# First conditioning on TensorE from eight 1 MB loads, and GpSimd without splits and tables, in a decoder block on one core

## The chip, the cores and the metric

The kernel runs on one core of a Trainium2 chip. The metric is the device time of one execution in microseconds. A core has five engines that run side by side and wait for one another by semaphores: TensorE (PE in the profile, its weight loads PEld), VectorE (DVE), ScalarE (ACT), GpSimd (POOL) and SyncE (SP, which here only issues loads and stores). Each engine works through its own instructions in order. DMAs are issued from the queues of SP, ACT and POOL and are carried out by 16 shared DMA engines.

## The reference, cut to what matters

One decoder layer for 256 tokens of width 1024, everything in float32:

```
mod = silu(c) @ ada_w + ada_b                 # c: 1 row of 1024; ada_w: 1024 x 6144
shift1, scale1, gate1, shift2, scale2, gate2 = split(mod, 6)
h = rms_norm(x, norm1_g) * (1 + scale1) + shift1
proj = h @ w_in + b_in                        # w_in: 1024 x 4384
# q, kv, gates, x_m, o_pre, i/f, merge gates = split(proj)
# three attention branches over compressed, selected and window keys:
#   s = q k * 0.125 - slope * dist, slope = 2**-(head+1); softmax; gated sum
# a chunked mLSTM with causal convolution
mixed = (g_a * (o_nsa @ proj_a) + g_b * (y_ml @ proj_b)) @ w_out
x = x + gate1 * mixed
h2 = rms_norm(x, norm2_g) * (1 + scale2) + shift2
x = x + gate2 * experts(h2)                   # top 4 of 32, clamped SwiGLU, 12 MB of weights each
out = rms_norm(x, final_g)
```

The compressed branch adds a position table `cmp_pe` to blocks of 32 keys and feeds them through `w1`, gelu and `w2`.

## The kernel before, in words

The program has two stages. The **block stage** computes everything up to the routing, the **expert stage** streams the weights of all 32 experts (each in 8 tiles of 128 x 2048 for the up projection and 4 for the down projection, 1 MB each, `fetch`) through 14 buffers and multiplies them with up to 64 gathered tokens an expert. A run-time branch for experts with more tokens stands behind it and is not taken here. Some 11 expert tiles are fetched already while the block stage ends (the list `FETCH`, by round).

**Conditioning (lines 149 to 238, 986 to 1013).** The first third of `mod` (shift1 and scale1, 2048 columns) is needed before the first product. It is computed in four quarters of 256 columns each of shift and scale (`ada_quarter(b)`): eight DMAs of 256 KB a quarter bring `ada_w`, DVE accumulates weight rows times `sc = silu(c)` over eight instructions (lines 209 and 211) into `aacc`, and eight matmuls with a 128 x 128 tile of ones as the weights sum over the partitions into columns (`ada_columns`). DVE then makes `mod` and `ab` (lines 222, 224), ACT makes two of the eight blocks of `h` transposed (`rows_T`, lines 232, 233; the normalized x lies transposed in PSUM), and DVE their low parts (line 237). Quarter b thus releases product b of the first pass.

**Products by parts.** A float32 product is made of three products in the faster fp32r form: a weight tile `w` is split into `r` (rounded, ACT, line 297 or 306) and the rest `l` (line 298 or 307, on DVE, or on POOL for the steps in `POOL_SPLIT`), activations into `hh` and `hl`; `mm3` (line 49) issues r x hh, l x hh, r x hl. A *step* is one 512 KB weight tile: a load (`s_load`, 5 buffers `w`), a split (`s_split`, one step ahead), 24 matmuls of 256 columns (`s_prod`). There are 35 steps of `w_in` in nine passes (`x`, `tok`, `q`, `k`, `o`, four of merge gates), 8 of the merge (`proj_a`, `proj_b`), 8 of `w_out`.

**Beside the steps** run generators, each advanced by a piece per step: `th_mlstm`, `th_cmp` (compressed keys), eight `th_att` (POOL first multiplies the tables `neg0` and `neg1` by the slope of each head, lines 898 and 899; DVE adds them to the scores and takes the row maximum, line 913), and `th_ada` (lines 538 to 587), which computes the other four sixths of `mod` (gate1, shift2, scale2, gate2: `q4` 0 to 3): 8 tiles `wada` of 512 KB each, two buffers, one `scalar_tensor_tensor` on DVE a tile (line 570), a tile fetched when the buffer two before is free; then two matmuls with ones sum over the partitions.

**What sets the order.** In the conditioning, ACT, DVE, SP and PE follow the written order (`manual_schedule`); POOL and everything behind it are ordered by a scheduler before the run. The small rows (`row_loads`: biases, norms, convolution weights, `cmp_pe`) are issued on ACT's queue in three portions.

Of the kernel before, what the change touches and what calls it, by code (L numbers as in the profile page):

```python
# [29 lines left out]
DIRECT = 0  # L30
ADA_POOL = ()
POOL_SPLIT = {0, 1, 2, *range(5, 60, 6)}
# [3 lines left out]
def block_kernel(ctx, tc, x, c, ada_w, ada_b, norm1_g, w_in, b_in, cmp_pe_k, cmp_w1_k, cmp_w2_k,  # L36
# [32 lines left out]
    mid2 = mixed.enter_context(tc.tile_pool(name="mid2", bufs=1))  # L69
# [38 lines left out]
    for h in range(2):  # L108
        SP.dma_start(xn[:, h, :], x[0, h * 128:(h + 1) * 128, :])
# [25 lines left out]
    def load_rows(n):  # L135
        for dst, src in row_loads[:n]:
            ACT.dma_start(dst, src)
        del row_loads[:n]
# [18 lines left out]
    def conditioning():  # L157
        tp = bank_m()
        PE.transpose(tp[:, 0:8], c8, ident[:8, :8])
        ACT.activation(sg8, tp[:, 0:8], AF.Sigmoid)  # L160
        DVE.tensor_tensor(sc, sg8, tp[:, 0:8], op=OP.mult)

# [18 lines left out]

    def columns(src, r0, r1, c0):
# [5 lines left out]
    accs, last_w = {}, {}  # L188
    spare = mid2.tile([128, 4, 1024], F32, name="spare", tag="gm")

    def ada_quarter(b):
        acc = accs[b] = mid.tile([128, 2, 256], F32, name="aacc", tag=("gate1", "shift2")[b % 2])
        for j in range(4):
            if j < 2:
                w = wtile()
            elif b in (1, 2):
                w = spare[:, (b - 1) * 2 + j - 2]
            else:
                w = mid.tile([128, 1024], F32, name="wada", tag="wada", bufs=2)
            w = w.rearrange("p (f a n) -> p f a n", f=2, a=2)  # L200
            for hf in range(2):
                c0 = hf * 1024 + b * 256
                SP.dma_start(w[:, hf], ada_w[0, j * 256:(j + 1) * 256, c0:c0 + 256].rearrange("(a p) n -> p a n", p=128))
            for a in range(2):
                kt = j * 2 + a
                if kt >= KT - DIRECT:
                    last_w[b, kt] = w[:, :, a]
                elif kt == 0:
                    DVE.tensor_scalar(acc, w[:, :, a], sc[:, 0:1], None, op0=OP.mult)
                else:  # L210
                    DVE.scalar_tensor_tensor(acc, w[:, :, a], sc[:, kt:kt + 1], acc, op0=OP.mult, op1=OP.add)
            yield

    def ada_columns(b):
        p = bank_o() if b % 2 else bank_m()
        parts = [(last_w[b, kt], sc[:, kt:kt + 1]) for kt in range(KT - DIRECT, KT)] + [(accs[b], ones[:, 0:1])]
        for i, (src, v) in enumerate(parts):
            for f in range(2):
                for k in range(2):
                    mm(p[:, f * 2 + k:f * 2 + k + 1], src[:, f, k * 128:(k + 1) * 128], v, i + f + k == 0, i == DIRECT)  # L220
        ks = slice(b * 2, b * 2 + 2)
        DVE.tensor_tensor(mod[:, b], p[:, 0:4].rearrange("p (f k) -> p f k", f=2),
                          col[:, R_ADA:R_ADA + 16].rearrange("p (f k) -> p f k", f=2)[:, :, ks], op=OP.add)
        DVE.scalar_tensor_tensor(ab[:, ks], mod[:, b, 1], 1.0, col[:, R_N1 + b * 2:R_N1 + b * 2 + 2],
                                 op0=OP.add, op1=OP.mult)

    def rows_T(b):
        hTs = []
        for kt in (b * 2, b * 2 + 1):
            src = xps[kt // 2][:, (kt % 2) * 256:(kt % 2) * 256 + 256]  # L230
            hT = mid.tile([128, S], F32, name="hT", tag="hT", bufs=3)
            ACT.activation(hT, src, AF.Identity, bias=mod[:, b, 0, kt % 2:kt % 2 + 1], scale=ab[:, kt:kt + 1])
            ACT.activation(hh[:, kt, :], hT, AF.Copy)
            hTs.append(hT)
        yield
        for kt in (b * 2, b * 2 + 1):
            DVE.tensor_tensor(hl[:, kt, :], hTs[kt % 2], f32(hh[:, kt, :]), op=OP.subtract)
        yield
# [28 lines left out]
    cbias = prol.tile([128, 2, 8, 15], F32, name="cbias")  # L267
    for h in range(8):
        cs = prol.tile([128, 2, 15], F32, name="cs", tag="cs", bufs=2)
        POOL.tensor_scalar(cs, cv, 2.0 ** -(h + 1), None, op0=OP.mult)  # L270
        POOL.tensor_tensor(cbias[:, :, h, :], cs, cneg, op=OP.add)
# [497 lines left out]
    def th_cmp():  # L769
# [10 lines left out]
        for i in range(2):  # L780
# [3 lines left out]
            POOL.memset(blk[:, :, 30:32], 0.0)  # L784
            kT = kvT[:, i, :]
            for g in range(2):
# [895 lines left out]
```

## Time and profile before

| | us |
|---|---|
| median of 3 runs | 1264.95 |
| lowest and highest | 1259.71, 1265.89 |
| the profiled execution, as timed | 1260.78 |
| its span, first to last instruction | 1259.0 |
| mean granted TensorE clock | 0.979 |
| bytes read from HBM | 462.09 MB, 369 GB/s over the span |

The span lies 1.8 us under its execution's own time. A busy PE in the profile is not a PE at its peak, since matmuls are pipelined and their ends are modelled; so the rate of the DMA engines, and what an engine waited for, say more than the busy shares. Idle time of an engine that nobody waits for costs nothing.

### The profile page before, as it was taken

Reading aid. Unit: us, or ns where it says so; the run is one execution under the profiler, and the core shown is the slowest. Engines: PE = TensorE matmul, PEld = TensorE weight load, DVE = VectorE, ACT = ScalarE, POOL = GpSimd, SP = SyncE. Lnnn points to the kernel's source line nnn. Section 1 sums busy time; section 2 is a strip of 40 time slices with the busy share of each in tenths; the row PEclk is TensorE's granted clock in tenths of the full one; section 3 lists DMA queues with packets and bytes.
Section 4 is the critical chain, followed back from the end, with each engine's and each line's share of the span. In section 5 each row is a group of like instructions: output and inputs, shape, how many; then the busy total and the mean of one; then the engine's idle time right before and its main releaser. Section 6 shows DMA issues by size and latency. Waiting matters only on the chain. (4 is left out here: it accounts for less than half of the span.)

```text
span 1259.0 us, 13889 instructions
## 1 busy us (share of the span) xinstructions
PE 1139.9 (91%) x5520; PEld 537.6 (43%) x5520; DVE 391.2 (31%) x775; ACT 251.7 (20%) x477; POOL 96.9 (8%) x112
## 2 busy tenths in 40 slices
PE   3788998988999999989998999999899989998976
PEld 2787887875333334323432333333234323432222
DVE  6787795853211131112111111211121212111112
ACT  3354556431201111000100110101001100101001
POOL 6501441100000000000000000000000000000020
PEclk9898998998999999999999999999999999999999
DMA  9697737886999999999999999999999999999994
GB/s 321 171 300 237 218 104 226 301 341 252 403 419 417 418 419 418 420 421 420 419 417 419 417 419 421 420 419 419 419 420 420 420 419 418 419 419 420 423 414 177
DMA packets 116590, 465.17 MB, mean 369 GB/s; under 512 B 11442, under 2 KB 37672, under 8 KB 83624
## 3 DMA queue, kind: packets, MB, share of 16 engines
q1 hardware_dynamic: 113600, 462.20, 92.7%
q10 hardware_dynamic: 2488, 1.45, 0.4%
q0 software_dynamic: 432, 0.58, 0.3%
q8 instruction: 45, 0.74, 0.2%
q14 instruction: 25, 0.20, 0.0%
HBM read 462.09 MB, written 2.10 MB: 369 GB/s over the span
## 5 line engine op out<-in xcount | busy, mean ns | idle before, releaser
L47 PE MATMUL psup<-ww,xg 128*64 128x512 f32 x2048 | 486.4, 602 | 25.3 <-DMA ww<-in_exp_w_up 24.9
L47 PE MATMUL psdn<-ww,a 128*64 128x512 f32 x1024 | 263.5, 605 | 27.3 <-DMA ww<-in_exp_w_down 27.2
L47 PEld LDWEIGHTS psup<-ww,xg 128*64 128x64 f32 x2048 | 142.4, 136 | 322.4 <-issue 226.6
L1407 DVE TENSOR_TENSOR g<-psgt,bup 128x512 f32<-128x512 f32 x32 | 22.1, 691 | 578.3 <-PE psgt L1390 562.8
L47 PEld LDWEIGHTS psdn<-ww,a 128*64 128x64 f32 x1024 | 81.8, 138 | 182.7 <-issue 117.6
L1383 ACT ACTIVATE gu<-psup 128x512 f32<-128x512 f32 x64 | 38.3, 598 | 347.0 <-PE psup L47 347.0
L1450 DVE TENSOR_TENSOR acc<-acc,psms 128x512 f32<-128x512 f32 x56 | 38.5, 688 | 162.6 <-PE psms L47 162.6
L47 PE MATMUL psf<-hh,r 128*128 128x256 f32 x256 | 81.6, 321 | 7.1 <-ACT gm L367 5.8
L47 PE MATMUL psf<-hh,l 128*128 128x256 f32 x256 | 76.8, 301 | 0.6 <-POOL l L298 0.6
L47 PE MATMUL psf<-hl,r 128*128 128x256 f32 x256 | 76.3, 299 | 0.0
L1475 POOL TENSOR_TENSOR acc<-acc,gate 128x512 f32<-128x512 f32 x4 | 5.0, 1262 | 869.1 <-DVE acc L1450 869.1
L47 PE MATMUL psms<-G,h 128*128 128x256 f32 x256 | 66.5, 405 | 0.2 <-DVE G L1275 0.2
L47 PE MATMUL psms<-y,sc 128*128 128x512 f32 x112 | 63.0, 645 | 0.0
L47 PEld LDWEIGHTS psms<-G,h 128*128 128x128 f32 x256 | 48.2, 198 | 30.5 <-issue 24.3
L47 PEld LDWEIGHTS psf<-hh,r 128*128 128x128 f32 x256 | 52.9, 207 | 12.6 <-ACT gm L367 6.1
L1409 ACT ACTIVATE s<-g 128x512 f32<-128x512 f32 x32 | 20.2, 632 | 187.7 <-DVE g L1408 187.7
L297 ACT ACTIVATE r<-w 128x1024 fp32r<-128x1024 f32 (+2 forms) x47 | 49.2, 1046 | 42.0 <-PE psf L47 24.4
L47 PEld LDWEIGHTS psf<-hh,l 128*128 128x128 f32 x256 | 53.1, 207 | 2.7 <-issue 1.4
L47 PEld LDWEIGHTS psf<-hl,r 128*128 128x128 f32 x256 | 52.8, 206 | 0.0
L298 DVE TENSOR_TENSOR l<-w,r 128x1024 fp32r<-128x1024 f32 (+2 forms) x36 | 44.8, 1245 | 13.6 <-ACT r L297 13.2
L570 DVE SCALAR_TENSOR_TENSOR ada<-wada,sc,ada 128x1024 f32<-128x1024 f32 x32 | 41.2, 1288 | 7.7 <-DMA wada<-in_ada_w 6.6
L1313 ACT ACTIVATE xg<-psms 128x512 f32<-128x512 f32 x32 | 19.1, 598 | 111.3 <-PE psms L47 111.3
(355 smaller groups left out, 972.4 us busy)
## 6 DMA issues: line engine op xcount, KB each, us to landing
ww<-in_exp_w_up SPq DMA_DIRECT2D x256, 1024.0 KB, 19.7
ww<-in_exp_w_down SPq DMA_DIRECT2D x126, 1024.0 KB, 19.9
wada<-in_ada_w SPq DMA_DIRECT2D x32, 512.0 KB, 4.8
w<-in_w_in SPq DMA_DIRECT2D x28, 512.0 KB, 4.5
w<-in_ada_w SPq DMA_DIRECT2D x16, 256.0 KB, 4.9
w<-in_w_out SPq DMA_DIRECT2D x8, 512.0 KB, 9.3
wada<-in_ada_w SPq DMA_DIRECT2D x8, 256.0 KB, 4.7
spare<-in_ada_w SPq DMA_DIRECT2D x8, 256.0 KB, 4.2
```

The costliest lines, as they stand in the source:

```text
L47: PE.matmul(o, a, b, start=start, stop=stop, skip_group_check=True)
L297: ACT.activation(r, w, AF.Copy)
L298: (POOL if at["split"] in POOL_SPLIT else DVE).tensor_tensor(l, w, f32(r), op=OP.subtract)
L570: DVE.scalar_tensor_tensor(a, w, sc[:, kt:kt + 1], a, op0=OP.mult, op1=OP.add)
L1313: ACT.activation(XG[g][:, q * 2:q * 2 + 2].rearrange("p k e s -> p (k e s)"), p, AF.Copy)
L1383: ACT.activation(GU[e][:, b], UP[e][b], AF.Copy)
L1407: DVE.tensor_tensor(by_f(g), by_f(GT[e][0]), bias(0), op=OP.add)
L1409: ACT.activation(s, g, AF.Sigmoid, scale=1.702)
L1450: DVE.tensor_tensor(acc[:, h, ns], acc[:, h, ns], p, op=OP.add)
L1475: POOL.tensor_tensor(acc[:, h, ns], acc[:, h, ns], gate2[:, ns], op=OP.mult)
```

## The change

Nine edits:

1. The first third of the conditioning moves from DVE to PE. Eight loads of 1 MB, each 128 rows of `ada_w` x 2048 columns (8 KB in a row), go to four buffers of a pool of their own, `st`, which is closed before the pool `mid2` is opened in its place (so `gm`, `xm` and `sgo` are made later, behind the conditioning). For each, four matmuls with `sc32` (one column of `sc` repeated 32 times, 128 x 32 weights) and 512 columns of the tile go into the four 32-row parts of one PSUM bank (`ada_rows`); after eight loads, ACT and DVE copy the bank out, four PE transposes turn it, and two DVE instructions give all of `mod` and `ab` at once (`ada_columns`). All of it then stands ahead of the first product.
2. The normalized x is copied from PSUM into SBUF (`xT`), and `row_T` makes `hh` on ACT and `hT` and `hl` on DVE.
3. x is loaded by one DMA in place of two.
4. Of the small rows, two stay on ACT's queue; nine go to POOL's queue.
5. The weights `wqk` and `w2t` are issued by SP in place of ACT.
6. `POOL_SPLIT` is empty: all splits run on DVE.
7. `ADA_POOL = (3,)`: for gate2's eight tiles, ACT scales the tile in place and POOL adds it to the sum, in place of one DVE instruction.
8. The slopes leave the tables: q is scaled by 0.125 / slope as it leaves PSUM (`qsc`), the tables are added unscaled, and the slope is a constant of the DVE instruction that adds; POOL's 32 multiplications of `neg0` and `neg1` go, as do its 16 small ones for `cbias` (in their place 16 tiny memsets; two small DVE multiplications in `th_cmp`).
9. In `th_cmp`, the blocks of keys are copied by ACT (eight copies), the position table becomes a 31st column of the same matmuls, and DVE adds its result afterwards.

```diff
-DIRECT = 0
-ADA_POOL = ()
-POOL_SPLIT = {0, 1, 2, *range(5, 60, 6)}
+ADA_POOL = (3,)
+POOL_SPLIT = ()
...
-    for h in range(2):
-        SP.dma_start(xn[:, h, :], x[0, h * 128:(h + 1) * 128, :])
+    SP.dma_start(xn, x[0].rearrange("(h p) d -> p h d", p=128))
...
+    def ada_load(kt):
+        w = st.tile([128, 2, 1024], F32, name="w1", tag="w1", bufs=4)
+        SP.dma_start(w.rearrange("p f n -> p (f n)"), ada_w[0, kt * 128:(kt + 1) * 128, 0:2048])
+        ada_w1.append(w)
+
+    def ada_rows(p, kt):
+        for f in range(2):
+            for n in range(2):
+                r0 = (f * 2 + n) * 32
+                mm(p[r0:r0 + 32, :], sc32[:, kt], ada_w1[kt][:, f, n * 512:(n + 1) * 512], kt == 0, kt == 7)
+
+    def ada_columns(p):
+        rw1 = mid.tile([128, 512], F32, name="rw1", tag="gain2")
+        ACT.activation(rw1[:, 0:256], p[:, 0:256], AF.Copy)
+        DVE.tensor_copy(rw1[:, 256:512], p[:, 256:512])
+        tp = bank_m()
         for j in range(4):
...
+            PE.transpose(tp[:, j * 128:(j + 1) * 128], rw1[:, j * 128:(j + 1) * 128], ident)
...
+    def row_T(kt):
+        src = xT[0][:, kt, :]
+        hT = mid.tile([128, S], F32, name="hT", tag="hT", bufs=3)
+        ACT.activation(hh[:, kt, :], src, AF.Identity, bias=mod[:, 0, kt:kt + 1], scale=ab[:, kt:kt + 1])
+        DVE.tensor_scalar(hT, src, ab[:, kt:kt + 1], mod[:, 0, kt:kt + 1], op0=OP.mult, op1=OP.add)
+        DVE.tensor_tensor(hl[:, kt, :], hT, f32(hh[:, kt, :]), op=OP.subtract)
...
-                    DVE.tensor_tensor(blkv[lp * 64:(lp + 1) * 64, :, g, :], src, pe_, op=OP.add)
+                    ACT.activation(blkv[ls, :, g, :], src, AF.Copy)
+                pe_ = col[ls, 128 + i * 32:160 + i * 32].rearrange("p (l r) -> p l r", r=2)[:, :, lp]
+                DVE.tensor_copy(blk[ls, :, 30], pe_)
...
-        for g in range(2):
-            sl = 2.0 ** -(g * 4 + cc + 1)
-            POOL.tensor_scalar(p0[:, g], neg0, sl, None, op0=OP.mult)
-            POOL.tensor_scalar(p1[:, g], neg1, sl, None, op0=OP.mult)
...
-                DVE.tensor_tensor_reduce(out=pp[:, g], in0=psg[g][:, (0, 128)[h]:(128, 384)[h]], in1=pp[:, g],
-                                         scale=1.0, scalar=FMIN, op0=OP.add, op1=OP.max,
+                DVE.tensor_tensor_reduce(out=pp[:, g], in0=psg[g][:, (0, 128)[h]:(128, 384)[h]], in1=(neg0, neg1)[h],
+                                         scale=2.0 ** -(g * 4 + cc + 1), scalar=FMIN, op0=OP.add, op1=OP.max,
                                          accum_out=m4[:, h, g:g + 1])
...
+        load_rows(2, ACT)
+        for kt in range(4):
+            ada_load(kt)
         conditioning()
         norm_sums()
...
+        ada_kt(0)
+        ada_kt(1)
         norm_rows()
...
+        load_rows(len(row_loads), POOL)
+        for kt in range(2, KT):
+            ada_kt(kt)
         columns(rows, 0, R_X, 0)
+        for _ in range(PW):
+            s_load()
+        ada_columns(p1)
```

(`ada_kt(kt)` is `ada_rows(p1, kt)` and, for kt under 4, the load kt + 4 behind it; `sc32` is made by one DVE copy; the branch for `q4 in ADA_POOL` stood in `th_ada` before.)

PE at the start of the program, before. `psm<-ones,aacc` are the sums over partitions of a quarter, `psf<-hh,r` begins the product that the quarter releases, `psa<-ident,xn` are the transposes of x:

```order
L159 MATMUL psm<-ident,raw 128x8
L178 MATMUL psa<-ident,xn 128x128 x16
L184 MATMUL pso<-ident,raw 128x24
L47 MATMUL psm<-ones,aacc 128x1 x4
L47 MATMUL pso<-ones,aacc 128x1 x4
L47 MATMUL psf<-hh,r 128x256
L47 MATMUL psf<-hh,l 128x256
```

PE at the same place now (`w_162` to `w_253` are the eight tiles `w1`, `sc_86` is `sc32`, `rw_286` the bank that is turned):

```order
L159 MATMUL psm<-ident,raw 128x8
L46 MATMUL psf<-w_162,sc_86 32x512 x4
L46 MATMUL psf<-w_164,sc_86 32x512 x4
L179 MATMUL psa<-ident,xn 128x128 x16
L46 MATMUL psf<-w_166,sc_86 32x512 x4
...
L46 MATMUL psf<-w_253,sc_86 32x512 x4
L195 MATMUL pso<-ident,raw 128x24
L218 MATMUL psm<-ident,rw_286 128x128 x4
L46 MATMUL psf<-hh,r 128x256
L46 MATMUL psf<-hh,l 128x256
```

Two of the eight groups stand ahead of the transposes of x and six behind them, and no product stands between two quarters any more: the first waits for all eight loads.

SP's queue at the start, before:

```order
L109 DMA xn<-in_x 128x1024 x2
L203 DMA w<-in_ada_w 128x2x256 x4
L203 DMA wada<-in_ada_w 128x2x256 x4
L286 DMA w<-in_w_in 128x2x512
L203 DMA w<-in_ada_w 128x2x256 x4
L203 DMA spare<-in_ada_w 128x2x256 x4
L286 DMA w<-in_w_in 128x2x512
```

and now:

```order
L108 DMA xn<-in_x 128x2x1024
L203 DMA w_162<-in_ada_w 128x2048
L203 DMA w_164<-in_ada_w 128x2048
...
L203 DMA w_253<-in_ada_w 128x2048
L279 DMA w<-in_w_in 128x2x512 x4
L368 DMA w<-in_w_in 128x3x128
```

The first weight tiles of `w_in` moved behind all of the conditioning's loads; the last four of those wait for a free buffer at the head of the queue.

ACT in the merge, before (`sT` turns shift2, `mh` are high parts of the merged rows):

```order
L297 ACTIVATE r<-w 128x1024 x2
L1189 ACTIVATE sT<-psa 128x512
L61 ACTIVATE mh<-mt_2477 128x256
L1189 ACTIVATE sT<-psa 128x512
L61 ACTIVATE mh<-mt_2483 128x256
L297 ACTIVATE r<-w 128x1024 x2
```

and now:

```order
L290 ACTIVATE r<-w 128x1024 x2
L1190 ACTIVATE sT<-psa 128x512
L60 ACTIVATE mh<-mt_2411 128x256
L1190 ACTIVATE sT<-psa 128x512
L557 ACTIVATE wada<-wada,sc 128x1024
L60 ACTIVATE mh<-mt_2417 128x256
L290 ACTIVATE r<-w 128x1024
L557 ACTIVATE wada<-wada,sc 128x1024
```

The scaling of gate2's tiles now stands between the splits of ACT, each behind the landing of its tile; the eight additions stand together on POOL.

## Rows read from the trace of the kernel before

**Rows 1.** The page's part 2: 40 slices of the span, GB/s.
```profile
GB/s 321 171 300 237 218 104 226 301 341 252 403 419 417 418 419 418 420 421 420 419 417 419 417 419 421 420 419 419 419 420 420 420 419 418 419 419 420 423 414 177
```

**Rows 2.** Busy time by stage: stretch, us, engines with instructions, granted clock, DMA share, GB/s.
```profile
0.00:55.60 55.60, 29.12 (x148) 27.27 (x148) 38.84 (x67) 18.55 (x33) 35.47 (x63) 0.91 0.78 245
...
120.00:217.00 97.00, 89.20 (x718) 78.48 (x719) 75.28 (x237) 56.59 (x135) 29.68 (x26) 0.95 0.61 185
217.00:285.30 68.30, 60.70 (x471) 55.84 (x470) 44.36 (x57) 29.18 (x49) 7.29 (x4) 1.00 0.85 309
...
300.00:1259.00 959.00, 895.85 (x3747) 318.51 (x3745) 171.12 (x291) 111.37 (x195) 12.50 (x10) 0.99 0.99 408
```

**Rows 3.** PE in order of time, first matmuls on expert weights (start us, us).
```profile
301.17 3.65 PE L47 MATMUL psup<-ww,xg 128*64 128x512 f32 x16
```

**Rows 4.** Who waited for whom, 0 to 55.6 us: total, times, longest.
```profile
ACT hT L232 <- DVE ab L224: 17.4, 4, 6.9
```

**Rows 5.** Stretches of 10 us in the conditioning, columns as in rows 2.
```profile
20.00:30.00 10.00, 2.41 (x11) 2.44 (x12) 8.76 (x14) 2.95 (x6) 2.34 (x1) 1.00 1.08 355
...
40.00:50.00 10.00, 7.31 (x39) 7.05 (x39) 7.27 (x10) 3.73 (x8) 7.49 (x11) 0.67 0.17 44
```

**Rows 6.** In order of time: x's second half squared, x transposed, a 32-column form.
```profile
6.29 1.06 ACT L167 ACTIVATE sq<-xn 128x1024 f32<-128x1024 f32 x1 [0.21 <-DMA xn<-in_x]
...
12.82 3.46 PE L178 MATMUL psa<-ident,xn 128*128 128x128 f32 x15 [0.57 <-ACT xn L172]
...
114.25 1.08 PE L47 MATMUL psa<-cw,blk 128*32 128x128 f32 x16
```

**Rows 7.** In order of time, the first pass: product 0 begins, product 3 ends.
```profile
29.28 0.56 PE L47 MATMUL psf<-hh,r 128*128 128x256 f32 x1
...
34.33 0.28 PE L47 MATMUL psf<-hl,r 128*128 128x256 f32 x1
...
50.34 0.42 DVE L237 TENSOR_TENSOR hl<-hT,hh 128x256 fp32r<-128x256 f32 x1 [0.43 <-ACT hh L233]
51.29 1.23 DVE L298 TENSOR_TENSOR l<-w,r 128x1024 fp32r<-128x1024 f32 x1 [0.52 <-ACT r L297]
...
52.25 0.28 PE L47 MATMUL psf<-hh,r 128*128 128x256 f32 x1
...
55.28 0.28 PE L47 MATMUL psf<-hl,r 128*128 128x256 f32 x1
```

**Rows 8.** DVE and POOL in order of time; the first row has no POOL beside it.
```profile
27.87 0.75 DVE L211 SCALAR_TENSOR_TENSOR aacc<-w,sc,aacc 128x512 f32<-128x512 f32 x1
...
41.64 5.14 DVE L211 SCALAR_TENSOR_TENSOR aacc<-wada,sc,aacc 128x512 f32<-128x512 f32 x4
42.29 2.37 POOL L298 TENSOR_TENSOR l<-w,r 128x1024 fp32r<-128x1024 f32 x1 [7.12 <-ACT r L297]
...
110.21 2.83 DVE L703 TENSOR_TENSOR k<-k,wcol 128x512 f32<-128x512 f32 x1
...
266.63 1.17 DVE L1135 TENSOR_TENSOR xt<-xt,xt 128x512 f32<-128x512 f32 x1
```

**Rows 9.** What PE waited for, 55 to 300 us: total, times, longest.
```profile
PE psf L47 <- POOL l L298: 3.4, 4, 1.3
...
PE psm L47 <- DVE k L703: 2.5, 1, 2.5
```

**Rows 10.** Groups by line, 55 to 290 us: busy us, mean ns, idle before.
```profile
L298 DVE TENSOR_TENSOR l<-w,r 128x1024 fp32r<-128x1024 f32 (+2 forms) x35 | 43.6, 1245 | 13.1 <-ACT r L297 12.7 <-DMA w<-in_proj_a 0.3
...
L298 POOL TENSOR_TENSOR l<-w,r 128x1024 fp32r<-128x1024 f32 (+1 forms) x8 | 21.2, 2656 | 100.0 <-ACT r L297 72.3 <-DVE ml L62 19.8 <-DVE wcol L702 7.9
```

**Rows 11.** gate2's first and last tile on DVE, in order of time (eight in all).
```profile
223.19 1.28 DVE L570 SCALAR_TENSOR_TENSOR ada<-wada,sc,ada 128x1024 f32<-128x1024 f32 x1 [1.09 <-DMA ada<-in_ada_b]
...
259.37 1.28 DVE L570 SCALAR_TENSOR_TENSOR ada<-wada,sc,ada 128x1024 f32<-128x1024 f32 x1
```

**Rows 12.** Tile wada, 186 to 262 us: its loads' time from issue to landing.
```profile
DMA to landing us min/median/max: 3.6/6.3/8.3
```

More of the change, by code (lines that the diff above doesn't have):

```diff
@@ L180, in norm_rows @@
             xps.append(p)
+        xT.append(keep.tile([128, KT, S], F32, name="xT", tag="x8"))
+        for k2 in range(4):
+            dst = xT[0][:, k2 * 2:k2 * 2 + 2].rearrange("p k s -> p (k s)")
+            if k2 % 2:
+                DVE.tensor_copy(dst, xps[k2])
+            else:
+                ACT.activation(dst, xps[k2], AF.Copy)
+    xT = []
     def columns(src, r0, r1, c0):
@@ L185, in columns @@
         ACT.activation(col[:, c0 + r0:c0 + r1], tp[:, r0:r1], AF.Copy)
[L188 to L192, printed above, removed]
-        for j in range(4):
[L194 to L238, printed above, removed]
+    ada_w1 = []
@@ L986, in block_kernel, with ada_kt @@
     with tc.manual_schedule(engines=START):
[L987 removed]
+        load_rows(2, ACT)
+        for kt in range(4):
+            ada_load(kt)
         conditioning()
         norm_sums()
[L990 removed]
+        p1 = bank_f()
+        def ada_kt(kt):
+            ada_rows(p1, kt)
+            if kt < 4:
+                ada_load(kt + 4)
+        ada_kt(0)
+        ada_kt(1)
         norm_rows()
[L992 to L994 removed]
+        load_rows(len(row_loads), POOL)
+        for kt in range(2, KT):
+            ada_kt(kt)
         columns(rows, 0, R_X, 0)
+        for _ in range(PW):
+            s_load()
+        ada_columns(p1)
         for b in range(4):
[L997 to L1013 removed]
+            if b == 0:
+                s_split()
+            for kt in (b * 2, b * 2 + 1):
+                row_T(kt)
+            if b:
+                s_split()
+                s_prod()
+        columns(rows, R_X, NR, 0)
+        columns(rows2, 0, 64, 128)
+        DVE.tensor_tensor(bq, col[:, R_Q:R_Q + 4], qsc, op=OP.mult)
     tc.no_sync_barrier()
+    first.close()
+    mid2 = mixed.enter_context(tc.tile_pool(name="mid2", bufs=1, reuse_waits="tile"))
     gm = mid2.tile([128, 16, S], F32, name="gm", tag="gm")
+    xm = mid2.tile([128, 4, 3 + S], F32, name="xm", tag="xm")
+    DVE.memset(xm[:, :, 0:3], 0.0)
+    sgo = mid2.tile([128, 4, S], F32, name="sgo")
     for i, wm in enumerate((ml_wq, ml_wk, ml_wv)):
[L1017 removed]
+        SP.dma_start(wqk[:, i], wm[0].rearrange("h d e -> d h e"))
     for i, w2 in enumerate((cmp_w2_k, cmp_w2_v)):
[L1019 removed]
+        SP.dma_start(w2t[:, i], w2[0])
     def ml_step(k):
```

73 lines of the change are left out of this document (29 added, 44 removed).

## The prediction

> **What bounds the kernel now.** I read the page's slices first. From the eleventh slice to the last but one the DMA engines bring 403 to 423 GB/s, and before that between 104 and 341 [rows 1]. The table by stage says the same in busy shares: from 300 to 1259 us the DMA share is 0.99 at 408 GB/s, and no engine but PE is busy for more than a fifth of it [rows 2]. So the expert stage runs at the speed of its loads, and nothing in this change touches its bytes. It begins when the routing is done: the first matmul on expert weights starts at 301.17 us [rows 3]. Its fetches are held by 14 buffers, so what the block stage saves or loses ahead of that moment goes into the end of the span one to one; 0 is my term for the expert stage itself. The forecast is therefore a forecast of the start at 301.17. What lies outside the span is 1260.78 - 1259.0 = 1.8 us, and stays.
>
> In the block stage I then looked for the wait that ends last. Up to 55.6 us DVE is busy for 38.84 us, and ACT waits 17.4 us in four waits for DVE's `ab` [rows 2, 4]: the first pass is paced by DVE's weighted sums, not by loads, for in the stretch from 40 to 50 us the DMA engines bring only 44 GB/s while DVE, PE and POOL each work about 7.3 us [rows 5]. From 120 to 217 us DVE is the busiest engine besides PE (75.28 of 97 us), and from 217 to 285.3 us it has 44.36 of 68.3 us [rows 2]. PE waits for little: 3.4 us for POOL's splits and 2.5 us for the `k` of DVE are the largest waits that have to do with POOL [rows 9].
>
> **A, the conditioning and the first pass.** Removed are DVE's 32 instructions of 128 x 512, 0.75 us each where POOL is quiet; four of them beside POOL's 2.37 us split took 5.14 us instead of 3.0 [rows 8]. So one POOL instruction there cost DVE 2.14 us. Added are loads and PE work, and I follow them in order of time. x was in SBUF by 6.3 us (the second square starts there, released by the load) [rows 6]. Behind it come 8 x 1.049 = 8.39 MB; at the expert stage's 408 GB/s [rows 2] that is 20.6 us, so 26.9. The last four loads wait at the head of SP's queue for a buffer that PE must have read; two of the eight groups stand ahead of x's transposes (3.46 us and more, from 12.82) and the rest behind [rows 6], which I put at 1 us of gap: 27.9. The last group is four matmuls of 32 x 512 side by side. The nearest row is 16 matmuls of 128 columns into 32-row parts in 1.08 us [rows 6], which is the same number of columns; the first product shows PE at the slower of its two levels after idle time (0.56 us a matmul at its start, 0.28 at its end) [rows 7], so I take 2.0: 29.9. Bank copies, four transposes and two small DVE instructions are six links; `hl` and its wait for ACT, 0.42 + 0.43, stand for two of them [rows 7], so 2.6: 32.5. The split's low part, 1.23, and the first `hT` and `hl` at about 0.42 each [rows 7] make 34.6. Then four products with no quarter between them: product 0 took 34.33 + 0.28 - 29.28 = 5.3 us and product 3 took 55.28 + 0.28 - 52.25 = 3.3 [rows 7], so 5.3 + 3 x 3.3 + 0.9 for the turning of `rows` between products 2 and 3 = 16.1. The pass ends at 50.7, against 55.56 before: **-4.8**.
>
> The bounds: at the 355 GB/s of the stretch from 20 to 30 us [rows 5], which is the best that the smaller loads reached, the bytes cost 3.0 more; and all four products at the slow level cost 3 x 2.0 = 6 more. In the stretch from 40 to 50 us, where products were cut off from each other by waits, the granted clock was 0.67, between the levels of 1.2 and 2.4 GHz [rows 5]; now they follow one another, so I don't take this, and leave +4 as the upper end. If the gap is nothing, the group costs 1.08 and every product 3.3, the end is 4 us earlier: -9. The range of A is -9 to +4.
>
> Moved at no cost, with their covers: nine small rows go to POOL's queue at about 15 us and are needed when `rows` is turned near 41 us, so 20 us and more cover them; `wqk` and `w2t` go behind the weight tiles on SP, where they are first used after the first pass; `gm`, `xm` and `sgo` now lie where the tiles `w1` lay, which are free some 20 us earlier; copying PSUM to `xT` lies under the loads. If a cover were gone, each is one load's time, 3.6 to 8.3 us for a 512 KB load [rows 12].
>
> **B, splits and tables leave POOL (55.6 to 285 us).** What PE waited for because of POOL is 3.4 us for `l` and 2.5 us for `k` [rows 9]. `k` took 2.83 us beside a split on POOL, where an instruction of the same size took 0.75 alone [rows 8], so 2.1 of the 2.5 is POOL's. That is 5.5 us. In return DVE takes eight splits of 1.245 us, 10.0 us, in place of POOL's 2.656 each [rows 10]. DVE is 78% busy from 120 to 217 [rows 2], so not all of this fits in gaps; but the products now get `l` 1.4 us sooner, and the eight copies of key blocks go to ACT, which has 40 us to spare there. I put back 1.5 of the 10: **-4**. The ends: nothing comes back, -6; six tenths of the 10 lie on the path while only the waits for `l` go, +3.
>
> **C, gate2 on ACT and POOL (217 to 285 us).** DVE loses eight instructions of 1.28 us, 10.2 us [rows 11]. POOL gains eight additions of the size of a split (2.37), with two inputs from SBUF. Each may hold DVE by 2.14 us, as the four sums show, or by as little as 1.17 - 0.75 = 0.42, as `xt` shows beside a split [rows 8]: 17.1 or 3.4 us, so DVE's sum changes by +6.9 or -6.8. ACT gains eight scalings of a 128 x 1024 tile, 1.06 each by x's square [rows 6], 8.5 us on an engine with 29.18 of 68.3 us busy [rows 2]. The two ends are equally far from zero and the rows equally near: **0**, with -6 to +7.
>
> The Trainium skill, page "SBUF — State Buffer", section "Who interferes with whom", says that a DVE instruction with two SBUF inputs contends with a GpSimd instruction that reads SBUF, and that the loser is blocked for the whole of the other's instruction. The four sums, 5.14 us for 3.0, agree with it; `xt` shows less than a whole one. By that rule C would stand at its upper end wherever DVE has such an instruction to run, and the whole sum at -2.
>
> **The sum.** -4.8 - 4 + 0 = -8.8 on the profiled execution's 1260.78: 1252.0. That execution lies 0.33% under the median of the three runs, so I say **1253**.
>
> **The rivals.** (a) Every relief passes whole: A -8, B -6, C -4, so 1243. For it: the rows of the first pass show DVE as the only thing waited for. Against: PE is busy for nine tenths of the stretch from 120 us [rows 2], and takes little of what is freed. (b) POOL's additions block DVE as the four sums were blocked, C is +6.9, and the start is as forecast: 1259, which is no change. For it: DVE has 44 us to run in that stretch and the additions 8 x 2.37 = 19 us. Against: only 65% of the stretch has a DVE instruction at all. The skill's page is this rival's rule.
>
> (c) Slower: gate2's tiles pace the block stage. A tile's buffer is now held from its load through ACT's scaling and POOL's addition, and there are two. The load takes 6.3 us in the middle and 8.3 at most [rows 12], the scaling 1.06 and the addition 2.37 with DVE's hold of 2.14 before it: 11.9 to 13.9 us, so 5.9 to 6.9 a tile. Before, eight tiles stood (259.37 - 223.19) / 7 = 5.2 us apart [rows 11]. The next load waits for its buffer at the head of SP's queue, with the `w` tiles of the steps behind it, and the scaling stands in ACT's queue ahead of the splits. At 6.9 that is 7 x 1.7 = 12 us, with rival b's 6.9 on top C is +19: 1271. It makes the kernel slower than the bound below when C passes 8.8 + 6.3 = 15, or at about 6.4 us a tile with the lock whole. Against: tiles are fetched ahead of the steps, and gate2 itself is needed only at the end. (d) The change doesn't do what it says: the four matmuls of a group run one behind another. Four times 1.08 to 2.0 us (by A) is 4.3 to 8.0 us a group against 2.6 us a load; at 6.2, eight groups from 9 us on end at 58 in place of 29.9: about 1280. Against it: 16 such matmuls of 128 columns took 1.08 us, where 15 transposes of 128 columns took 3.46 one behind another [rows 6].
>
> **How the numbers follow.** Forecast 0.48 (of it 0.38 faster by over 0.5%, 0.10 within), rival a 0.18 (faster), rival b 0.18 (within), rival c 0.10 and rival d 0.03 (slower), and 0.03 within for what I haven't named. 0.5% is 6.3 us, about what a measurement of this kernel can tell from no change. Faster 0.56, same 0.31, slower 0.13. The lower ends sum to -9 - 6 - 6 = -21, 1240; the upper to +14, 1275. Leaving out rival d and most of c above, and the last of a below, 1241 to 1265 holds 8 in 10.
>
> **What would show it.** A: DMA at 400 GB/s or more up to about 27 us, the first product near 35, the last of the four near 51; wrong, if the groups of four take over 3 us or PE keeps the slow level through the pass. B: no wait of PE for POOL, `k` at 0.75, and no new wait for DVE's `l` of more than 2 us. C: DVE's instructions beside POOL's additions tell rival b by their length; waits of ACT for `wada`, or of `w` loads behind it, tell rival c. The whole: the first expert matmul near 292 instead of 301.17, and everything behind it as long as before. The prediction is wrong altogether if the expert stage's own length changes.

## The result, and the profile after

The changed kernel takes 1249.95 us in the median of four runs (1248.24 to 1251.08), the kernel before 1264.62 in the same comparison: a ratio of 0.989, with a 95% interval from 0.9861 to 0.9919. That is 1.1% faster, 13.9 us by the ratio. The forecast was 1253, with 1241 to 1265. Its profiled execution took 1248.24 us with a span of 1246.0; against the profiled execution of before (1260.78) that is 12.5 us less. Each of the two lies under its own median.

The page's speed rows, 40 slices of the span, answer to [rows 1]: the plateau of the expert stage stands as high as it stood, and begins with the eleventh slice again, each slice being 0.3 us shorter now.

```profile
DMA  9798577958999999999999999999999999999994
GB/s 356 223 293 247 161 217 237 382 195 312 421 420 418 419 418 417 419 421 419 418 419 419 419 418 419 419 420 419 419 420 421 419 418 418 418 420 420 421 414 162
```

Busy time by stage (columns as in [rows 2]): the conditioning with the first pass, 97 us around the end of `w_in`, the last 70 us of the merge with `w_out`, the expert stage.

```profile
0.00:49.40 49.40, 32.42 (x184) 18.62 (x184) 18.61 (x47) 17.42 (x29) 20.09 (x60) 0.83 0.87 301
104.00:201.00 97.00, 92.75 (x791) 80.75 (x784) 80.19 (x255) 67.48 (x154) 3.00 (x5) 1.00 0.70 215
201.00:271.00 70.00, 58.20 (x446) 53.57 (x444) 44.73 (x49) 31.12 (x49) 21.53 (x8) 1.00 0.78 279
300.00:1246.00 946.00, 883.48 (x3686) 315.16 (x3682) 169.86 (x287) 106.93 (x185) 12.52 (x10) 0.99 1.00 410
```

DVE in the conditioning fell from 38.84 us of 55.6 to 18.61 of 49.4. PE is busy for 92.75 us of the second stretch, where it had 89.20 in a stretch of the same 97 us up to the end of `w_in` before (the second stretch passes that end, which is at 196.9, by 4 us). In the merge PE has 58.20 us of 70.0, where it had 60.70 of 68.3, and GpSimd 21.53, where it had 7.29. The expert stage brings 410 GB/s, where it had 408.

PE in order of time: the last of the conditioning's groups, the first product, the last matmul of the first pass, and the first matmuls on expert weights (start us, us), to be held against [rows 3, 7].

```profile
28.73 1.77 PE L46 MATMUL psf<-w,sc 128*32 128x512 f32 x8 [0.58 <-DMA w<-in_ada_w]
...
33.28 0.38 PE L46 MATMUL psf<-hh,r 128*128 128x256 f32 x1 [1.16 <-ACT hh L227]
...
49.15 0.28 PE L46 MATMUL psf<-hl,r 128*128 128x256 f32 x1
...
286.83 3.65 PE L46 MATMUL psup<-ww,xg 128*64 128x512 f32 x16
```

The expert stage begins 301.17 - 286.83 = 14.3 us earlier; the span is 13.0 us shorter, so the expert stage gave back 1.3. The table gives the same milestones for the kernels of the next section, from the trace of each: end of the first pass, of `w_in` and of `w_out` on PE, the first expert matmul, and the time as timed, with its ratio to the kernel before in the same comparison.

| kernel | first pass | `w_in` | `w_out` | expert | median us | ratio, 95% interval |
|---|---|---|---|---|---|---|
| before | 55.6 | 217.0 | 285.3 | 301.2 | 1264.62 | |
| after | 49.4 | 196.9 | 271.0 | 286.8 | 1249.95 | 0.9890 (0.9861 to 0.9919) |
| a_alone | 51.2 | 211.3 | 284.0 | 299.5 | 1257.50 | 0.9953 (0.9936 to 0.9971) |
| b_alone | 56.6 | 209.0 | 276.6 | 293.2 | 1252.49 | 0.9889 (0.9859 to 0.9918) |
| split_pool | 50.8 | 202.7 | 280.8 | 296.7 | 1256.07 | 0.9954 (0.9938 to 0.9970) |
| tables_pool | 49.5 | 202.5 | 277.6 | 293.2 | 1252.86 | 0.9923 (0.9897 to 0.9948) |
| no_split29 | 57.0 | 210.9 | 280.7 | 296.4 | 1259.66 | 0.9977 (0.9960 to 0.9995) |
| gate2_dve | 49.0 | 197.0 | 267.0 | 282.5 | 1241.43 | 0.9821 (0.9790 to 0.9852) |
| adds_memset | 49.7 | 198.8 | 263.4 | 277.6 | 1239.24 | 0.9811 (0.9783 to 0.9838) |
| add_twice | 48.8 | 194.2 | 278.8 | 295.3 | 1259.72 | 0.9968 (0.9950 to 0.9987) |
| warm | 48.8 | 197.2 | 266.1 | 281.7 | 1242.78 | 0.9841 (0.9815 to 0.9867) |
| blk_dve | 49.3 | 197.3 | 267.3 | 282.9 | 1242.62 | 0.9819 (0.9793 to 0.9844) |

A trace is one execution, and executions of one kernel spread by some 3 to 10 us; the milestones say where in the program something happens, the medians what it is worth. Microseconds between two kernels of the table are taken from their ratios, since each has its own runs of the kernel before beside it. The lead over the kernel before is 6.2 us at the end of the first pass, 20.1 at the end of `w_in`, and 14.3 at the end of `w_out`. So the first pass, which A is about, gained 6.2, the middle 13.9, and the merge gave 5.8 back.

### The profile page after: what moved, and what is told of

Its sections match the earlier page's. It is cut to its first block, busy times and chain, and to the rows that moved or that the text cites. A ratio compares the mean times of both kernels' runs of the same rounds, so it can differ in the third digit from the quotient of the medians.

```text
span 1246.0 us, 13896 instructions
## 1 busy us (share of the span) xinstructions
PE 1140.4 (92%) x5556; PEld 528.5 (42%) x5556; DVE 366.3 (29%) x752; ACT 262.7 (21%) x488; POOL 59.9 (5%) x87
## 5 line engine op out<-in xcount | busy, mean ns | idle before, releaser
L46 PE MATMUL psf<-hh,l 128*128 128x256 f32 x256 | 74.0, 290 | 1.4 <-DVE l L291 1.4
L291 DVE TENSOR_TENSOR l<-w,r 128x1024 fp32r<-128x1024 f32 (+2 forms) x47 | 56.9, 1211 | 17.2 <-ACT r L290 17.2
L46 PEld LDWEIGHTS psms<-G,h 128*128 128x128 f32 x256 | 48.2, 198 | 30.5 <-issue 24.3
L46 PEld LDWEIGHTS psf<-hh,r 128*128 128x128 f32 x256 | 50.2, 197 | 9.0 <-issue 4.5
L46 PEld LDWEIGHTS psf<-hh,l 128*128 128x128 f32 x256 | 50.3, 196 | 3.4 <-DVE l L291 1.8
L46 PEld LDWEIGHTS psf<-hl,r 128*128 128x128 f32 x256 | 50.1, 196 | 0.6 <-DVE hl L229 0.6
L1391 PEld LDWEIGHTS psgt<-ident,gu 128*128 128x128 f32 x256 | 27.4, 140 | 26.7 <-issue 24.3
```

What stands on the lines that cost most here:

```text
L46: PE.matmul(o, a, b, start=start, stop=stop, skip_group_check=True)
L291: (POOL if at["split"] in POOL_SPLIT else DVE).tensor_tensor(l, w, f32(r), op=OP.subtract)
L1391: PE.transpose(GT[e][b][:, j * 128:(j + 1) * 128], GU[e][:, b, j * 128:(j + 1) * 128], ident)
```

## The experiments

**The conditioning alone.** a_alone is the changed kernel with GpSimd loaded as before.

```diff
-ADA_POOL = (3,)
-POOL_SPLIT = ()
+ADA_POOL = ()
+POOL_SPLIT = {0, 1, 2, *range(5, 60, 6)}
...
+            POOL.tensor_scalar(p0[:, g], neg0, 1.0, None, op0=OP.mult)
+            POOL.tensor_scalar(p1[:, g], neg1, 1.0, None, op0=OP.mult)
```

> The changed kernel with GpSimd loaded as before: eight of the splits and the table multiplications on GpSimd again, gate2's eight tiles on one DVE instruction each. What is left is the conditioning on PE, the loads and the small edits. Theory 1 (the conditioning is worth 6.2 us, as its end at 49.4 in place of 55.6 us shows, and all the rest of the gain in the block stage comes from GpSimd's work): about 1258, ratio 0.995, with the stretch from 50 us on as long as before within 2 us, PE's long wait for gm near 200 us (5.8 us in the kernel before) back at the same place. Theory 2 (the earlier start alone loosens the later stalls, through loads that come earlier): 1250 or less, and the wait for gm gone.

By its median it is worth 0.47%, 5.9 us, as theory 1 said. Its trace, which is of the longest of its eight executions (1261.46), shows more: the lead of 4.4 us at the end of the first pass is gone two steps later. In order of time, POOL's last table multiplications, the split of step 5 behind them, and the matmul that waits for it:

```profile
52.06 0.94 ACT L290 ACTIVATE r<-w 128x864 fp32r<-128x864 f32 x1
...
56.93 0.55 POOL L891 TENSOR_SCALAR p<-neg 128x128 f32<-128x128 f32 x1
57.45 0.84 POOL L892 TENSOR_SCALAR p<-neg 128x256 f32<-128x256 f32 x1
58.25 0.62 POOL L1181 DMA_DIRECT2D rb<-in_router_b  x1
58.89 2.13 POOL L291 TENSOR_TENSOR l<-w,r 128x864 fp32r<-128x864 f32 x1
...
61.08 0.61 PE L46 MATMUL psf<-l,hh 128*128 128x288 f32 x1 [6.64 <-POOL l L291]
```

The high part `r` was done at 53.0, and GpSimd came to the low part at 58.9, because twelve table multiplications stood ahead of it in its queue from 47.7 us on. Before, the same multiplications ended at 56.1, and GpSimd then waited 1.15 us for `r`, so nobody waited for them. So a faster conditioning brings PE to a queue on GpSimd that is not done, and at that place the lead is lost. It isn't lost for good: PE's 5.8 us for `gm` did not come back in this trace, which theory 1 had wrong and theory 2 right, and at the end of `w_in` the lead is 5.7 us. In the merge this execution lost 4.4 us of it again (72.7 us for 68.3), with a granted clock of 0.83 from 240 to 250 us where the kernel before has 1.00 over its merge [rows 2]; so the worth of the conditioning is to be read from the median.

**GpSimd relieved alone.** b_alone is the kernel before, with its DVE conditioning, where all splits run on DVE and the slopes are out of the tables.

```diff
-POOL_SPLIT = {0, 1, 2, *range(5, 60, 6)}
+POOL_SPLIT = ()
...
-            POOL.tensor_scalar(p0[:, g], neg0, sl, None, op0=OP.mult)
-            POOL.tensor_scalar(p1[:, g], neg1, sl, None, op0=OP.mult)
...
-                                         scale=1.0, scalar=FMIN, op0=OP.add, op1=OP.max,
+                                         scale=2.0 ** -(g * 4 + cc + 1), scalar=FMIN, op0=OP.add, op1=OP.max,
```

> The kernel before with its DVE conditioning, but with all splits on DVE and the slopes out of the tables as in the change (GpSimd has neither); gate2 on DVE as it was, blocks of keys on DVE as they were. Theory 1 (taking splits and tables off GpSimd is worth most of the gain by itself, and the conditioning on PE adds its 6 us on top): 1246 to 1249, ratio 0.987 to 0.989; the first pass ends within 3 us of 55.6; no wait of PE for gm. Theory 2 (the two need each other: without PE's conditioning the DVE has no room for the splits): 1252 or more.

0.9889 is the ratio that theory 1 named, while the median lies 3.5 us over its microseconds and within those of theory 2. What theory 2 says, that there is no room on DVE without the other conditioning, doesn't hold: the first pass ended at 56.6, 1 us later, though three more splits ran on DVE, and of the wait for `gm` 0.2 us is left. Relieving GpSimd is worth 11.6 us by the medians (the kernel before took 1264.07 here) and 14 by the ratio, by itself, and the conditioning on PE, added to it (gate2_dve against b_alone, 0.9821 / 0.9889), another 8.7; the intervals do not tell this from the 5.9 of a_alone. So the two halves of the change add up within the intervals: 0.47% and 1.11% alone, 1.79% together (gate2_dve).

**The two reliefs apart.** split_pool puts only the splits back on GpSimd, tables_pool only the table multiplications.

```diff
-POOL_SPLIT = ()
+POOL_SPLIT = {0, 1, 2, *range(5, 60, 6)}
```

> The changed kernel with the old set of splits on GpSimd (every sixth step), tables and gate2 as in the changed kernel. Theory 1 (the splits on GpSimd cost PE their waits and the lock on DVE, 5 to 6 us of the gain, though without the table multiplications ahead of them they are no longer late): 1254 to 1257. Theory 2 (what cost the time was the queue of table multiplications ahead of a split, and the splits themselves only shift work): 1249 to 1251, no change.

```diff
+            POOL.tensor_scalar(p0[:, g], neg0, 1.0, None, op0=OP.mult)
+            POOL.tensor_scalar(p1[:, g], neg1, 1.0, None, op0=OP.mult)
...
-in1=(neg0, neg1)[h],
+in1=pp[:, g],
```

> The changed kernel with the 32 table multiplications on GpSimd again (the scores read the copies), the splits still on DVE. Theory 1 (the tables cost by what stands behind them on GpSimd, and no split stands there now): 1250 to 1253. Theory 2 (the table multiplications cost by themselves, by coming late for the scores and by slowing DVE): 1255 to 1258, about the share of B that the splits leave.

The splits cost 0.65%, 8 us: the time lies in theory 1's range, the price somewhat over its 5 to 6 us. At the end of `w_in` 5.8 us of it are there, and 4.0 more come in the merge, where splits and gate2's additions are then both on GpSimd; which of the two holds the other up there was not tried. The tables alone cost 0.33%, 4 us, with an interval that overlaps that of the changed kernel, so their share is not settled to better than a few microseconds; the milestones of the one trace say 5.6 us at the end of `w_in`. The median lies at the upper end of theory 1's range and under theory 2's; that the tables cost something without a split behind them is not shown by it.

**One late split.** In the list of PE's waits of the kernel before, the largest from 55 us on is not one of [rows 9]: it is 5.8 us, once, for ACT's `gm`. Followed back in that trace, row by row, in order of time:

```profile
182.35 2.18 POOL L899 TENSOR_SCALAR p<-neg 128x256 f32<-128x256 f32 x2
184.50 2.88 POOL L298 TENSOR_TENSOR l<-w,r 128x1024 fp32r<-128x1024 f32 x1
...
187.41 0.38 SPq L286 DMA_DIRECT2D w<-in_w_in  x1
187.88 0.89 SPq L551 DMA_DIRECT2D wada<-in_ada_w  x2
...
194.26 1.28 DVE L570 SCALAR_TENSOR_TENSOR ada<-wada,sc,ada 128x1024 f32<-128x1024 f32 x1 [4.09 <-DMA wada<-in_ada_w]
...
200.31 0.17 DVE L917 TENSOR_SCALAR m<-m 128x4 f32<-128x4 f32 x1
200.51 0.40 ACT L921 ACTIVATE p<-p,m 128x128 f32<-128x128 f32 x1 [2.99 <-DVE m L917]
200.91 1.55 ACT L367 ACTIVATE gm<-psf,col 128x256 f32<-128x256 f32 x4
201.79 0.58 PE L47 MATMUL psf<-hh,r 128*128 128x256 f32 x1 [5.84 <-ACT gm L367]
```

GpSimd's split stands behind its table multiplications and ends at 187.38. The load of the next weight tile needs that tile's buffer; it waits at the head of SP's queue and goes out at 187.41, and the `wada` load behind it at 187.88. DVE waits 4.09 us for `wada`, with the row maximum `m` behind; ACT waits for `m`, with `gm` behind; PE waits 5.84 us for `gm`. no_split29 takes that one split off GpSimd in the kernel before.

```diff
-POOL_SPLIT = {0, 1, 2, *range(5, 60, 6)}
+POOL_SPLIT = {0, 1, 2, *range(5, 60, 6)} - {29}
```

> The kernel before with a single split taken off GpSimd: that of step 29, which stood behind 9 us of table multiplications and ended at 187.4 us. Theory 1 (that one late split held the load of a weight tile at the head of SP's queue for 5.7 us, the wada load behind it came late, DVE waited 4.1 us for it ahead of a row maximum, ACT waited for that ahead of gm, and PE 5.8 us for gm): the wait for gm goes and the time falls by 4 to 6.5 us, to 1256 to 1259, ratio 0.996. Theory 2 (that stall belongs to DVE's load and to the order of its queue): within 1 us of the kernel before.

PE's waits from 55 to 300 us, its four largest (total, times, longest):

```profile
PE psf L47 <- DVE l L298: 5.5, 6, 2.4
PE psf L47 <- POOL l L298: 2.8, 3, 1.3
PE psm L47 <- DVE k L703: 2.5, 1, 2.5
PE psa L1149 <- DVE us L1136: 2.2, 1, 2.2
```

`gm` is no longer among them, `w_in` ends 6.1 us earlier and `w_out` 4.6, and the median falls by 0.23%, 2.9 us, with 0.6 to 5.1 by its interval. The chain is as theory 1 told it, for the wait went with the split, which theory 2 excluded. The gain is under theory 1's 4 to 6.5 us, whose lower part the interval still holds; in the same trace PE's waits for DVE's `l` are 5.5 us where they were 2.8, so part of the wait that went came back under another name.

**gate2.** gate2_dve puts gate2's tiles back on DVE in the changed kernel.

```diff
-ADA_POOL = (3,)
+ADA_POOL = ()
```

> The changed kernel with gate2's tiles back on one DVE instruction each (nothing on ACT and GpSimd). Theory 1 (GpSimd's additions hold DVE's instructions of the merge, and C costs the 5.8 us by which the lead over the kernel before shrinks from 20.1 to 14.3 us): about 1244, the DVE instructions of 128 x 256 in the merge back from 2.5 to 0.41 us, ratio to the kernel before 0.984. Theory 2 (the lead shrinks because DVE now makes all the splits of the merge, the additions are hidden): 1249 to 1252, as the changed kernel or slower, since DVE gets 10 us of work back.

It is faster than both kernels: 0.9821, an interval that does not meet that of the changed kernel. Against the changed kernel that is 0.7%, 8.7 us; the milestones show 4.0 us at the end of `w_out`, all of it lost in the merge (`w_in` ends at 197.0 and 196.9). In the changed kernel, DVE and POOL in order of time:

```profile
211.61 2.38 POOL L558 TENSOR_TENSOR ada<-ada,wada 128x1024 f32<-128x1024 f32 x1 [3.53 <-ACT wada L557]
211.80 2.47 DVE L61 TENSOR_TENSOR ml<-mt,mh 128x256 fp32r<-128x256 f32 x1 [1.04 <-ACT mh L60]
...
215.02 3.36 POOL L558 TENSOR_TENSOR ada<-ada,wada 128x1024 f32<-128x1024 f32 x1 [1.04 <-ACT wada L557]
...
216.07 2.60 DVE L451 TENSOR_TENSOR mt<-mt 128x256 f32<-128x256 f32 x1
...
218.70 0.42 ACT L60 ACTIVATE mh<-mt 128x256 fp32r<-128x256 f32 x1 [1.84 <-DVE mt L451]
```

The groups of `mt` and `ml` from 195 to 286 us (busy us, mean ns), first of the changed kernel, then of gate2_dve:

```profile
L451 DVE TENSOR_TENSOR mt<-mt 128x256 f32<-128x256 f32 x8 | 9.9, 1240 | 0.0
L61 DVE TENSOR_TENSOR ml<-mt,mh 128x256 fp32r<-128x256 f32 x8 | 7.5, 932 | 2.7 <-ACT mh L60 2.7
```

```profile
L451 DVE TENSOR_TENSOR mt<-mt 128x256 f32<-128x256 f32 x8 | 3.2, 419 | 0.0
L61 DVE TENSOR_TENSOR ml<-mt,mh 128x256 fp32r<-128x256 f32 x8 | 3.2, 419 | 0.0
```

Sixteen instructions took 17.4 us in place of 6.4. Each held instruction in the rows above ended 0.3 us after the addition beside it (211.80 + 2.47 against 211.61 + 2.38, 216.07 + 2.60 against 215.02 + 3.36): it lost the rest of the addition's time. They are the worst place for it: PE's next products wait for `mh` and `ml`, and DVE's next splits stand behind them. From the end of `w_in` to that of `w_out` PE waits 5.8 us for DVE's `l`, in gate2_dve 2.2. Two more kernels tell the addition's reading from the queues around it. In adds_memset GpSimd only writes:

```diff
-                    POOL.tensor_tensor(a, a, w, op=OP.add)
+                    POOL.memset(w, 0.0)
+                    POOL.memset(w, 0.0)
```

> The changed kernel with each of gate2's eight additions on GpSimd replaced by two memsets of the same tile, which only write and read nothing (gate2's sum is left out). ACT still scales each tile, GpSimd still holds each tile for about 2 us, and SP's queue waits for it as before. Theory 1 (the additions cost because they read SBUF beside DVE's instructions with two SBUF inputs): mt and ml of the merge back at 0.41 us, the time near that with gate2 on DVE, 1241 to 1244. Theory 2 (ACT's eight scalings and the held buffers cost, through the queues): 1248 to 1251, as the changed kernel.

```profile
L61 DVE TENSOR_TENSOR ml<-mt,mh 128x256 fp32r<-128x256 f32 x8 | 3.2, 420 | 1.0 <-ACT mh L60 1.0
L451 DVE TENSOR_TENSOR mt<-mt 128x256 f32<-128x256 f32 x8 | 3.2, 418 | 0.0
```

With ACT's scalings still there, the same two groups are back at 0.42 us each, and the time is that of gate2_dve (0.9811 against 0.9821). Four of the `mt` and a split (1.23 us) ran beside a memset; the other instructions of the two groups met none. What the kernel does not keep is the queue: SP's loads of `wada` waited 4.7 us for GpSimd from 190 to 271 us, and 17.0 in the changed kernel. gate2_dve settles that point. There the same loads waited 16.6 us, for DVE, and the kernel is the faster one; PE waits for no load in the merge of either. add_twice goes the other way:

```diff
                     POOL.tensor_tensor(a, a, w, op=OP.add)
+                    POOL.tensor_tensor(a, a, a, op=OP.subtract)
```

> The changed kernel with a second GpSimd instruction of two SBUF inputs (ada minus ada) behind each of gate2's additions; it doesn't hold the loaded tile longer (gate2's sum is left out by it). Theory 1 (each such instruction may hold one DVE instruction for about 2.1 us): 1254 to 1260, about twice as many DVE instructions of 2.5 us in the merge. Theory 2 (DVE has room, the cost lies in the queues): 1249 to 1251.

```profile
L451 DVE TENSOR_TENSOR mt<-mt 128x256 f32<-128x256 f32 x8 | 11.6, 1447 | 0.0
L61 DVE TENSOR_TENSOR ml<-mt,mh 128x256 fp32r<-128x256 f32 x8 | 11.4, 1429 | 2.1 <-ACT mh L60 2.1
```

23.0 us for the sixteen, and 9.8 us by the ratios, in the range of theory 1, with SP's `wada` loads waiting 19.7 us where they waited 17.0. Its count was too high: seven of the sixteen took 2.06 to 2.61 us and two 1.5, where five were held before. Only three of the eight second instructions found one of them to hold; DVE's splits were hit too, at 1.54 us in the mean in place of 1.25.

The Trainium skill, "SBUF — State Buffer", section "Who interferes with whom", has this rule: a DVE instruction with two SBUF inputs contends with a GpSimd instruction that reads SBUF, and not with one that only writes. The additions and the memsets agree with both halves, with 2.5 to 2.6 us against 0.42. That the loser is blocked for the whole of the other's instruction, which the prediction takes from the same section, stands there for DVE's two-port modes; here the held instructions lost what was left of the addition, 2.1 us.

**The clock in the conditioning.** In the changed kernel the granted clock was 0.61 from 20 to 33 us and 0.54 from 33 to 40.3 us, which is near the lower of the levels of 1.2 and 2.4 GHz, and the first product took 39.64 - 33.28 = 6.4 us (columns as in [rows 2]):

```profile
20.00:33.00 13.00, 8.61 (x37) 1.34 (x37) 1.23 (x4) 1.78 (x4) 1.55 (x3) 0.61 1.02 393
33.00:40.30 7.30, 6.68 (x29) 6.20 (x30) 6.31 (x14) 4.26 (x8) 0.00 (x0) 0.54 0.61 148
```

PE was busy for 8.61 of the first 13 us, waiting for a load before each group. warm (with gate2 on DVE) keeps PE at work between the groups.

```diff
+        pw = bank_f()
+        def warm(n):
+            for i in range(n):
+                PE.transpose(pw[:, i % 4 * 128:i % 4 * 128 + 128], ident, ident)
...
+            if kt >= 2:
+                warm(12 if kt < 7 else 2)
...
         ada_columns(p1)
+        warm(8)
```

> The changed kernel with gate2 on DVE, and with 70 transposes of ident into a PSUM bank that nobody reads, on PE between the groups of the conditioning and ahead of the first product. Theory 1 (PE comes to the first product at the lower clock because it waits between the groups): the granted clock from 20 to 40 us is 0.9 or more in place of 0.54 to 0.61, the first product takes about 3.5 us in place of 6.3, the first pass ends 3 to 4 us earlier, time 1237 to 1239. Theory 2 (the first product is paced by its operands, one block of h after another, whatever the clock): no change from gate2 on DVE alone, 1241 to 1243.

Busy time of warm in the two stretches (columns as in [rows 2]):

```profile
20.00:33.00 13.00, 12.42 (x99) 6.88 (x98) 0.42 (x1) 1.29 (x3) 2.10 (x3) 1.00 1.02 393
33.00:40.30 7.30, 5.76 (x43) 4.92 (x42) 6.58 (x15) 5.92 (x11) 0.00 (x0) 1.00 0.51 128
```

The clock was granted in full, as theory 1 said, and the time stayed where theory 2 put it: the first pass ended at 48.8 in place of 49.0. The clock itself was worth something. From the start of the eighth group to the end of the pass, warm took 18.7 us and gate2_dve 20.5; but the eighth group came at 30.1 us, 1.5 later than in gate2_dve and 1.4 later than in the changed kernel (its first group had come 0.8 us late already, and the added transposes stood right ahead of the eighth), and that took it back. Products 0 and 1 took 4.2 and 4.0 us where gate2_dve took 6.1 and 3.0, with waits for DVE's `l` and `hl` among their matmuls. At the full clock these two products are held up by DVE, which makes `l`, `hT` and `hl` in turn; products 2 and 3 waited for neither.

**The blocks of keys.** blk_dve takes edit 9's copies from ACT to DVE, gate2 on DVE.

```diff
-                    ACT.activation(blkv[ls, :, g, :], src, AF.Copy)
+                    DVE.tensor_copy(blkv[ls, :, g, :], src)
```

> The changed kernel with gate2 on DVE, and the eight copies of key blocks on DVE in place of ACT. Theory 1 (DVE's 4.6 us for them lay beside other work, ACT's copies bring nothing): 1240 to 1243, as with gate2 on DVE alone. Theory 2 (they stood on the path, at the place near 110 us where the step of 9.5 us became one of 4.3): 1245 to 1247.

No change from gate2_dve (0.9819 against 0.9821): theory 1.

## Why the prediction was right, and which of its terms were not

The direction was right and the time lies in the range: 1253 forecast, 1249.95 measured, and the bound and its consequence held. The start of the expert stage moved by 14.3 us where 9 were forecast (286.8 against 292), and the expert stage ran on as long as before but for 1.3 us. The sum was too small, -8.8 us for 13.9 by the ratio and 12.5 between the two profiled executions, and it came no further off because two of its terms were wrong in opposite directions. That 1253 is so near is luck also in the last step: 1252.0 was worked out for the profiled execution, and with the 0.33% by which that lies under its median it would have been 1256.

**A held, in size and in most of its steps.** -6.2 against -4.8. The loads came at 393 to 424 GB/s after 16 us (306 to 319 before), the last group began at 28.7 and ended at 30.5 (forecast 29.9), the links to the first product took 2.8 us where 4.7 was summed (PE began when `hh` was there, not `l` and `hl`), product 0 took 6.4 for 5.3, and the pass ended at 49.4 (50.7). Groups of four took 1.94 us at the lower clock: the estimate of 2.0 was good, and rival d is out. What A did not say is that its lead runs into GpSimd's tables two steps later, where a_alone waits 6.6 us; by its median A alone is still worth 5.9.

**B was mis-sized: -13.9 for -4, and outside its own range of -6 to +3.** The step that failed is the first one, "what PE waited for because of POOL". It took the waits whose releaser was named POOL, and `k`. The largest wait in that list, 5.8 us for ACT's `gm`, was passed over, although five links back it was a GpSimd split that held SP's queue. The experiment without that split shows it. The wait is not B's alone, though: it is also gone in a_alone, with splits and tables on GpSimd. Nor is all of the middle's gain B's: b_alone has 9.0 us of it there (209.0 - 56.6 = 152.4 for 161.4), a_alone 1.3, and the remaining 3.6 came only with both, or lie in the spread between executions. The upper-cost side failed too, in b_alone: DVE's 10 us of splits were to give back 1.5 us, but PE's waits for `l` there are 3.5 us in all, where they were 2.8 for DVE's and 3.4 for POOL's. In the changed kernel they are 7.2:

```profile
PE psf L46 <- DVE l L291: 7.2, 8, 1.8
PE psm L46 <- DVE xc L595: 4.0, 2, 2.5
```

None is longer than 1.8 us, as the prediction asked. The waits of [rows 9] for POOL's `l` and for `k` went as forecast: `k` took 0.69 us in the changed kernel at 100.95. The rest of the 13.9 is not split up by the runs to better than a few microseconds: splits alone cost 8 us, tables alone 4, each put back by itself.

**C was mis-sized: +4.0 at the end of `w_out` for 0, inside its range of -6 to +7.** Of the 5.8 us of lead that the merge gave back, 4.0 come again in gate2_dve, with gate2 on DVE; the other 1.8 do not, and are not C's. The step that failed is "the rows equally near": between the hold of 2.14 us and the 0.42 of `xt`, the first was the nearer. Of the eight additions five held one of `mt` or `ml` for 2.1 us each (2.47, 2.60, 2.61, 2.63 and 2.48 us for 0.41), and DVE has these on PE's path. Rival b was therefore true of C, with 4.0 us at the end of `w_out` and 8.7 by the ratios against gate2_dve, beside a gain in B that rival b did not have. Rival c's queue did fill, but it does not tell the kernels apart: SP's `wada` loads waited 17.0 us in the changed kernel and 16.6 in gate2_dve.

The edits costed at nothing cost nothing that can be seen: PE waits nowhere for the small rows or for `wqk` and `w2t`. No run takes them back one by one.

## What to carry to other kernels

A wait that a profile charges to one engine has to be followed back until it reaches work that nobody waits for: an in-order queue (here SP's, then DVE's, then ACT's) passes a late buffer on under other names, and the sum over waits with the right name, 5.5 us, was well under half of the 13.9 that came. Work on GpSimd that reads SBUF was not free here for GpSimd being idle: its price was what it held on DVE, and the price counted where DVE's two-input instructions lay on the path. And when a first stage gets faster, ask which queue was quietly filling under it.

## What the runs showed of the hardware that was not expected

- A granted clock of 1.00 at the start of a trace need not be a measurement. In the stretch from 29 to 35 us the row of the kernel before says 1.00, and yet matmuls of 256 columns stood 0.21 us apart up to 34.1 us. The changed kernel had the same 0.21 us at a granted clock of 0.54, and 0.12 us at 0.99 (40.3 to 50 us). The trace's own record of the granted clock begins at 34.2 us in the kernel before and at 13.1 in the changed one; what lies ahead of it is counted as 1.00. So the prediction was right to read the lower level off the length of the matmuls, and the clock that the tables by stage give for the conditioning (0.91 and 0.83) is too high by what isn't on record. The stretch, and two of its matmuls, of the kernel before:

```profile
29.00:35.00 6.00, 5.69 (x28) 5.50 (x28) 5.24 (x8) 3.04 (x6) 2.19 (x1) 1.00 1.05 338
```

```profile
30.07 0.41 PE L47 MATMUL psf<-hh,r 128*128 128x256 f32 x1
30.28 0.41 PE L47 MATMUL psf<-hh,l 128*128 128x256 f32 x1
```

- GpSimd's own instruction grows with the hold: 3.36 us for an addition that took 2.37 where DVE left it alone, and 3.24 in three places of add_twice. Either side can lose: where the addition took 3.36 us, DVE's split had begun 0.1 us ahead of it and took its usual 1.22.
- Four matmuls of 32 columns of weights and 512 of data, into the four 32-row parts of one bank, ran side by side: 1.07 us for a group at the full clock (granted 0.99 to 1.00), up to 1.94 at the lower (0.50 to 0.58). The trace's 64 records of them last 0.94 us each in the mean, 60 us in sum, in 13.6 us of PE's time; all of it lies under loads that took 27.
